# A masked-patch loss: batch sums by a 32x32 transposition and a store from four partitions, in place of a mask product

## The chip, the cores and the metric

The kernel runs on one core of a Trainium2 chip. Its engines are named as in the profile: PE (TensorE), DVE (VectorE), ACT (ScalarE), POOL (GpSimd) and SP (SyncE, which here only issues transfers). The metric is the device time of one execution in microseconds; a profile of one execution also gives the span from the first to the last instruction, which is a little shorter.

## The reference

`pred` and `target` are 32 x 147 x 768 in f32. Each row of 768 of `target` is normalised by its own mean and variance; the result is, for each of the 32 batch elements, the mean over 147 rows and 768 columns of the squared difference.

```python
mean = target.mean(axis=-1, keepdims=True)
var = target.var(axis=-1, keepdims=True)
target = (target - mean) / np.sqrt(var + 1e-6)
loss = np.mean((pred - target) ** 2, axis=-1)
return loss.mean(axis=-1).astype(np.float32)
```

## The kernel before

The rows lie on 128 partitions: partition 4*b + j holds a stretch of batch element b, so J = 4 partitions belong to one element. 147 rows are not divisible by 4: j = 0, 1, 2 hold 37 rows and j = 3 holds 36. In the code's terms a "column" c is one row of 768 on each partition; columns 0 to 35 fill 128 partitions, and the column REST = 36 exists for j = 0, 1, 2 alone and is kept packed on 96 partitions, three for each element.

Loads come in pieces, in a fixed order. The first four columns of `target` and its REST column go through SP's hardware queue in f32; all others go through POOL's software queue, which converts to bf16 on the way. `target`'s REST column is cut into five transfers:

```python
if c0 == REST and kind == "t":
    for j, b0, b1 in [(j, 0, B) for j in range(J - 2)] + [(J - 2, 0, 16), (J - 2, 16, 24), (J - 2, 24, B)]:
        pin(eng.dma_start(out=til[:n].rearrange("(b j) w -> b j w", j=J - 1)[b0:b1, j],
                          in_=bass.AP(tensor=x.tensor, offset=src.offset + b0 * N * D + j * KJ * D,
                                      ap=[[N * D, b1 - b0], [1, w]])))
else:
    pin(eng.dma_start(out=til[:n], in_=src))
```

For each column DVE takes the statistics (L164, L165), ACT the root (L188), DVE the reciprocal (L194), POOL the normalised target `s` (L214). Then the difference is formed, either by PE (minus identity times `s`, plus identity times `pred`, into PSUM, L231) or by DVE (L276), and squared and summed along the row by ACT (L260) or DVE (L280). Each such unit leaves one f32 number per partition:

```python
pin(nc.scalar.activation(out=z[:n, :w], in_=z[:n, :w], func=ACTF.Square, accum_out=dest[:n]))
...
pin(nc.vector.scalar_tensor_tensor(out=z, in0=z, scalar=1.0, in1=z, op0=ALU.mult, op1=ALU.mult, accum_out=dest))
```

The sums of the 22 early units are columns of one tile `rl`, which DVE reduces; REST's sum and those of the six last units stand alone (`finals`). PE then adds everything up across partitions: eight accumulating f32 products with a mask of 128 x 32 (96 x 32 for REST) whose entries are 1/(N*D) where the partition belongs to the element, else 0. The last of these comes when the last unit is done; the sums lie in one partition of PSUM, and are copied and stored.

```python
nc.gpsimd.memset(m, 1.0 / (N * D))          # masks(): the same for mask and mask_rest, each with
nc.gpsimd.affine_select(...)                # two selections that set the rest to 0
...
acc = psum1.tile([1, B], F32)
op("rl_sum", "DVE", 0.2, early_ops, lambda: pin(nc.vector.tensor_reduce(
    out=rl_sum, in_=rl, axis=mybir.AxisListType.X, op=ALU.add)), rank=3.0)
finals.insert(0, ("rl_sum", rl_sum, mask, P))
...
    pin(nc.tensor.matmul(acc, vec[:n], m[:n], start=len(turn) == 1, stop=len(turn) == len(finals)))
...
ob = singles.tile([1, B], F32)
pin(nc.vector.tensor_copy(out=ob, in_=acc))
nc.sync.dma_start(out=out, in_=ob[0, :])
```

The masks and identities are made by POOL at the start, ahead of its first loads. All operations are listed with estimated durations, and a small scheduler in the kernel's Python fixes their order on each engine.

Of the kernel before, what the change touches and what calls it, by code (L numbers as in the profile page):

```python
# [7 lines left out]
F32 = mybir.dt.float32  # L8
BF16 = mybir.dt.bfloat16
ALU = mybir.AluOpType  # L10
ACTF = mybir.ActivationFunctionType
# [3 lines left out]
def kernel(  # L15
# [7 lines left out]
    nc = tc.nc  # L23
    pin = tc.keep_in_program_order
    B, N, D = pred.shape
    eps = 1e-6
    P = 128
    J = P // B
    KJ = (N + J - 1) // J
    KM = N - (J - 1) * KJ  # L30
    assert KJ == KM + 1
    RP = B * (J - 1)
    half = D // 2
    BANK = 512
    REST = KM
# [4 lines left out]
    def rows_of(c):  # L40
        return RP if c == REST else P
# [5 lines left out]
    singles = ctx.enter_context(tc.tile_pool(name="singles", bufs=1))  # L47
    psum1 = ctx.enter_context(tc.tile_pool(name="psum1", bufs=1, space=bass.MemoryType.PSUM))

    stream = []
# [40 lines left out]
    def op(name, engine, dur, needs, fn, rank=0.0, early=0.0):  # L93
        by_name[name] = len(ops)
        ops.append((name, engine, dur, needs, fn, rank, early))
# [4 lines left out]
    def load(kind, c0, c1, d0, d1, q):  # L100
        x = targ_f if kind == "t" else pred_f
        n, w = rows_of(c0), d1 - d0
        til = data.tile([P, (c1 - c0) * w], BF16 if q == "sw" else F32, name=f"{kind}{c0}_{d0}")
        src = bass.AP(tensor=x.tensor, offset=x.offset + c0 * D + d0,
                      ap=[[N * D, B], [KJ * D, J - 1 if c0 == REST else J], [1, (c1 - c0) * w]])
        eng = {"hw": nc.sync, "hw2": nc.scalar, "sw": nc.gpsimd}[q]
        if c0 == REST and kind == "t":

            for j, b0, b1 in [(j, 0, B) for j in range(J - 2)] + [(J - 2, 0, 16), (J - 2, 16, 24), (J - 2, 24, B)]:
                pin(eng.dma_start(out=til[:n].rearrange("(b j) w -> b j w", j=J - 1)[b0:b1, j],  # L110
                                  in_=bass.AP(tensor=x.tensor, offset=src.offset + b0 * N * D + j * KJ * D,
                                              ap=[[N * D, b1 - b0], [1, w]])))
        else:
            pin(eng.dma_start(out=til[:n], in_=src))  # L114
        for c in range(c0, c1):
            KIND[kind].setdefault(c, []).append((d0, d1, til, (c - c0) * w))


    land, lanes, clock = {}, {"hw": [], "hw2": [], "sw": []}, 2.3
    for i, (kind, c0, c1, d0, d1, q) in enumerate(stream):  # L120
        w = (c1 - c0) * (d1 - d0)
        clock += w * rows_of(c0) / P * 0.915 / D + (0.0 if w >= 4 * D else 0.04)
        lanes[q].append(clock + 1.1)
        for c in range(c0, c1):
            land[kind, c, d0] = clock + 1.1
        k = len(lanes[q])
        op(("load", i), {"hw": "SP", "hw2": "ACT", "sw": "POOL"}[q], 0.6, [], lambda a=stream[i]: load(*a), rank=-1.0,
           early=0.0 if k <= 8 else lanes[q][k - 9] + 0.3)

    def landed(kind, c):  # L130
        return max(t for (k, cc, d), t in land.items() if k == kind and cc == c)

    ident = singles.tile([P, P], BF16)
    nident = singles.tile([P, P], BF16)
    mask = singles.tile([P, B], F32)
    mask_rest = singles.tile([P, B], F32)
    eps_t = singles.tile([P, 1], F32)

    def identities():
# [3 lines left out]
                                        base=0, pattern=[[-1, P]], channel_multiplier=1))  # L143

    def masks():
        for m, per, n in ((mask, J, P), (mask_rest, J - 1, RP)):
            pin(nc.gpsimd.memset(m, 1.0 / (N * D)))
            pin(nc.gpsimd.affine_select(out=m[:n], in_=m[:n], compare_op=ALU.is_ge, fill=0.0,  # L148
                                        base=0, pattern=[[-per, B]], channel_multiplier=1))
            pin(nc.gpsimd.affine_select(out=m[:n], in_=m[:n], compare_op=ALU.is_ge, fill=0.0,  # L150
                                        base=per - 1, pattern=[[per, B]], channel_multiplier=-1))

    op("eps", "DVE", 0.1, [], lambda: pin(nc.vector.memset(eps_t, eps)))
    op("ident", "POOL", 1.3, [], identities, rank=-2.0)
# [50 lines left out]
    def normalise(u, c):  # L205
        n = rows_of(c)
        if c == u[0]:
            s = work.tile([P, 2 * D], BF16, name="s")
            for m, cc in enumerate(u):
                sbuf[cc] = (s, m * D)  # L210
        s, so = sbuf[c]
        (_, _, til, o), = tbuf[c]
        r, nm = rs[c]
        pin(nc.gpsimd.tensor_scalar(out=s[:n, so:so + D], in0=til[:n, o:o + D], scalar1=nm, scalar2=r,  # L214
                                    op0=ALU.add, op1=ALU.mult))
# [41 lines left out]

    def square_act(u, d0, w, dest):
        n, z = rows_of(u[0]), zs[u, d0]
        pin(nc.scalar.activation(out=z[:n, :w], in_=z[:n, :w], func=ACTF.Square, accum_out=dest[:n]))  # L260

    def difference(u, d0, w):

# [13 lines left out]

    def square_dve(u, d0, w, dest):
        z = zs[u, d0][:, :w]
        pin(nc.vector.scalar_tensor_tensor(out=z, in0=z, scalar=1.0, in1=z, op0=ALU.mult, op1=ALU.mult,  # L280
                                           accum_out=dest))

    tail = 6
    n_early = len(units) - 1 - tail
    rl = singles.tile([P, n_early], F32)
    rl_sum = singles.tile([P, 1], F32)
    pairs_pe = [u for u, d0, d1, eng in units if eng == "ACT" and (u[0] == REST or len(u) * (d1 - d0) > 2 * BANK)]
    n_pairs = len(pairs_pe)
# [2 lines left out]
    finals = []  # L291
    early_ops, users, dusers, dprev, pusers, lusers, seen = [], [], [], [], [], [], set()
    for k, (u, d0, d1, eng) in enumerate(units):
        w = len(u) * (d1 - d0)
        arrive = max(t for (kk, c, d), t in land.items() if kk == "p" and c in u and d < d1)
        norms = [("norm", c) for c in u]
        for c in u:
            if c not in seen:
                op(("norm", c), "POOL", 1.02, [("recip", group_of[c])], lambda u=u, c=c: normalise(u, c), rank=k)
                seen.add(c)  # L300
        if k < len(units) - tail:
            if u[0] == REST:
                dest = singles.tile([P, 1], F32, name="rl_rest")
                finals.append((("sq", k), dest, mask_rest, RP))
            else:
                dest = rl[:, len(early_ops):len(early_ops) + 1]
                early_ops.append(("sq", k))
        else:
            dest = singles.tile([P, 1], F32, name=f"rl{k}")
            finals.append((("sq", k), dest, mask, P))  # L310
        if eng in ("DVE", "DVE+ACT"):
            op(("diff", k), "DVE", 0.57 * w / D + 0.05, norms + dusers[-5:-4] + dprev[-1:], lambda u=u, d0=d0, w=w: difference(u, d0, w), rank=-2.0,
               early=arrive)
            dusers.append(("sq", k))
            dprev.append(("diff", k))
            if eng == "DVE":
                op(("sq", k), "DVE", 1.0 * w / D, [("diff", k)],
                   lambda u=u, d0=d0, w=w, dest=dest: square_dve(u, d0, w, dest), rank=-1.0)
            else:
                op(("sq", k), "ACT", 0.65 * w / D + 0.22, [("diff", k)],  # L320
                   lambda u=u, d0=d0, w=w, dest=dest: square_act(u, d0, w, dest), rank=k)
            continue
        op(("subt", k), "PE", 0.37 * w / D, norms + (users[-2:-1] if len(users) < n_pairs else users[n_pairs - 1:n_pairs] + (pusers[-2:-1] if wide(u) else lusers[-3:-2])) + ["ident"],
           lambda u=u, d0=d0, w=w: sub_target(u, d0, w), rank=k + 0.0)
        op(("pred", k), "PE", 0.37 * w / D, [("subt", k)], lambda u=u, d0=d0, w=w: add_pred(u, d0, w), rank=k,
           early=arrive)
        op(("sq", k), "ACT", 0.65 * w / D + 0.22, [("pred", k)],
           lambda u=u, d0=d0, w=w, dest=dest: square_act(u, d0, w, dest), rank=k)
        users.append(("sq", k))
        if len(users) > n_pairs:  # L330
            (pusers if wide(u) else lusers).append(("sq", k))

    acc = psum1.tile([1, B], F32)
    op("rl_sum", "DVE", 0.2, early_ops, lambda: pin(nc.vector.tensor_reduce(
        out=rl_sum, in_=rl, axis=mybir.AxisListType.X, op=ALU.add)), rank=3.0)
    finals.insert(0, ("rl_sum", rl_sum, mask, P))
    turn = []

    def final(vec, m, n):
        turn.append(n)  # L340
        pin(nc.tensor.matmul(acc, vec[:n], m[:n], start=len(turn) == 1, stop=len(turn) == len(finals)))  # L341


    for i, (need, vec, m, n) in enumerate(finals):
        op(("final", i), "PE", 0.2, [need, "masks"], lambda v=vec, m=m, n=n: final(v, m, n), rank=90.0,
           early=max(land.values()) + 0.4)


    HOP = 0.15
# [3 lines left out]
    while left:  # L353
        best = None
        for i in left:
            name, engine, dur, needs, fn, rank, early = ops[i]
            if any(x not in end for x in needs):
                continue
            t = max([free[engine], early] + [end[x] + (0.0 if ops[by_name[x]][1] == engine else HOP) for x in needs])
# [4 lines left out]
        _, i, t = best  # L364
        name, engine, dur, needs, fn, rank, early = ops[i]
# [2 lines left out]
        order.append((t, name, engine))  # L368
        fn()

    ob = singles.tile([1, B], F32)
    pin(nc.vector.tensor_copy(out=ob, in_=acc))  # L372
    nc.sync.dma_start(out=out, in_=ob[0, :])


# [33 lines left out]
```

## Time and profile before

| | |
|---|---|
| device time, median of 3 | 76.61 us (76.5 to 76.67) |
| span of the profiled execution | 75.0 us |
| busy: DVE, POOL, ACT, PE | 55.9, 52.5, 30.7, 28.3 us |
| DMA | 15.41 MB written by the transfers, 28.90 MB read from HBM |
| mean granted clock of PE | 0.923 |

A busy time is the sum over an engine's instructions, whatever they wait for; the share of the span that it makes says how much room an engine has on average. The slices show when an engine or the DMA is busy, and the chain that ended last follows the work back from the last instruction, each time to what released it.

### The profile page before, as it was taken

Reading aid. Unit: us, or ns where it says so; the run is one execution under the profiler, and the core shown is the slowest. Engines: PE = TensorE matmul, PEld = TensorE weight load, DVE = VectorE, ACT = ScalarE, POOL = GpSimd, SP = SyncE. Lnnn points to the kernel's source line nnn. Section 1 sums busy time; section 2 is a strip of 40 time slices with the busy share of each in tenths; the row PEclk is TensorE's granted clock in tenths of the full one; section 3 lists DMA queues with packets and bytes.
Section 4 is the critical chain, followed back from the end, with each engine's and each line's share of the span. In section 5 each row is a group of like instructions: output and inputs, shape, how many; then the busy total and the mean of one; then the engine's idle time right before and its main releaser. Section 6 shows DMA issues by size and latency. Waiting matters only on the chain.

```text
span 75.0 us, 567 instructions
## 1 busy us (share of the span) xinstructions
PE 28.3 (38%) x87; PEld 8.7 (12%) x88; DVE 55.9 (74%) x154; ACT 30.7 (41%) x65; POOL 52.5 (70%) x72
## 2 busy tenths in 40 slices
PE   0000003570000000398940006897860560789650
PEld 0000000110000000123300002142220210222120
DVE  0000899999999999970899999860997579999850
ACT  5100022202002020059502020878969979985960
POOL 5899008995299939499869995982798799950000
PEclk9999999999999999999999999999999955555796
DMA  0799999999999999999999989999999999999900
GB/s 0 236 420 346 233 215 220 192 231 223 229 210 210 214 200 220 223 236 229 216 223 216 208 174 213 216 226 216 216 213 210 197 219 210 213 202 207 140 0 0
DMA packets 3301, 15.41 MB, mean 206 GB/s; under 512 B 418, under 2 KB 1154, under 8 KB 2786
## 3 DMA queue, kind: packets, MB, share of 16 engines
q0 software_dynamic: 2992, 13.52, 88.5%
q1 hardware_dynamic: 306, 1.87, 6.7%
q14 instruction: 3, 0.02, 0.1%
HBM read 28.90 MB, written 0.00 MB: 385 GB/s over the span
## 4 chain that ended last, share of the span: by engine, by line
DMA 79%; POOL 7%; ACT 5%; PE 4%; issue 1%; DVE 0%; ACTq 0%; POOLq 0%
DMA t<-in_target_dram 43%; DMA p<-in_pred_dram 36%; PE zp L231 4%; POOL t L114 3%; ACT zl L260 2%; ACT zp L260 2%; POOL p L114 1%; POOL nident L142 0%; POOL ident L142 0%; PE acc L341 0%; POOL mask L148 0%; POOL mask_rest L148 0%; POOL mask L150 0%; POOL mask_rest L150 0%; DVE ob L372 0%
## 5 line engine op out<-in xcount | busy, mean ns | idle before, releaser
L214 POOL TENSOR_SCALAR s<-t,nm,r 128x768 bf16<-128x768 bf16 (+2 forms) x37 | 39.0, 1062 | 7.1 <-DVE r L194 6.6
L164 DVE BATCH_NORM_STATS2 st<-t 128x6 f32<-128x384 bf16 (+2 forms) x74 | 36.2, 531 | 7.6 <-DMA t<-in_target_dram 7.5
L231 PE MATMUL z<-p,ident 128*128 128x512 bf16 (+2 forms) x25 | 9.3, 509 | 21.5 <-DMA p<-in_pred_dram 21.5
L231 PE MATMUL z<-s,nident 128*128 128x512 bf16 (+2 forms) x26 | 10.5, 522 | 15.2 <-POOL s L214 13.8
L188 ACT ACTIVATE r<-mv,eps_t 128x4 f32<-128x4 f32 (+2 forms) x11 | 3.2, 295 | 31.1 <-DVE mv L165 30.2
L260 ACT ACTIVATE z<-z 128x1536 f32<-128x1536 f32 (+1 forms) x9 | 12.3, 1364 | 8.1 <-PE z L231 8.1
L114 POOL DMA_DIRECT2D p<-in_pred_dram x15 | 8.5, 570 | 6.1 <-DMA t<-in_target_dram 3.9
L276 DVE TENSOR_TENSOR zd<-p,s 128x1536 bf16<-128x1536 bf16 (+3 forms) x13 | 8.6, 680 | 2.1 <-DMA p<-in_pred_dram 2.0
L165 DVE BATCH_NORM_AGGREGATE mv<-st 128x2 f32<-128x12 f32 (+1 forms) x37 | 7.7, 209 | 1.3
L231 PEld LDWEIGHTS <-ident 128*128 128x128 bf16 (+1 forms) x36 | 4.6, 127 | 34.1 <-issue 32.8
L260 ACT ACTIVATE zd<-zd 128x1536 bf16<-128x1536 bf16 (+1 forms) x5 | 6.7, 1345 | 0.6 <-DVE zd L276 0.5
L231 PEld LDWEIGHTS <-nident 128*128 128x128 bf16 (+1 forms) x36 | 3.6, 115 | 28.4 <-issue 16.8
L280 DVE SCALAR_TENSOR_TENSOR zd<-zd 128x256 bf16<-128x256 bf16 (+2 forms) x8 | 5.3, 662 | 0.2
L194 DVE RECIPROCAL r<-r 128x4 f32<-128x4 f32 (+2 forms) x11 | 1.5, 133 | 4.5 <-ACT r L188 4.5
L260 ACT ACTIVATE zp<-zp 128x1024 f32<-128x1024 f32 (+1 forms) x4 | 3.6, 899 | 1.1 <-PE zp L231 1.1
L231 PE MATMUL zp<-p,ident 128*128 128x512 bf16 x7 | 3.5, 581 | 0.9 <-DMA p<-in_pred_dram 0.9
L231 PE MATMUL zp<-s,nident 128*128 128x512 bf16 x7 | 2.7, 484 | 2.5 <-ACT z L260 2.5
L114 POOL DMA_DIRECT2D t<-in_target_dram x6 | 3.6, 623 | 0.0
L231 PE MATMUL zl<-s,nident 128*128 128x512 bf16 x3 | 1.8, 585 | 3.5 <-POOL s L214 3.5
L189 ACT ACTIVATE nm<-mv 128x4 f32<-128x4 f32 (+2 forms) x11 | 2.1, 189 | 0.0
L260 ACT ACTIVATE zl<-zl 128x512 f32<-128x512 f32 x3 | 1.8, 585 | 0.0
L231 PE MATMUL zl<-p,ident 128*128 128x512 bf16 x3 | 1.6, 531 | 0.4 <-DMA p<-in_pred_dram 0.4
(29 smaller groups left out, 10.5 us busy)
## 6 DMA issues: line engine op xcount, KB each, us to landing
t<-in_target_dram POOLq DMA_DIRECT2D x4, 768.0 KB, 13.4
t<-in_target_dram POOLq DMA_DIRECT2D x2, 1536.0 KB, 27.1
p<-in_pred_dram POOLq DMA_DIRECT2D x4, 768.0 KB, 38.7
t<-in_target_dram SPq DMA_DIRECT2D x1, 1536.0 KB, 6.9
p<-in_pred_dram POOLq DMA_DIRECT2D x1, 1536.0 KB, 38.7
p<-in_pred_dram POOLq DMA_DIRECT2D x4, 384.0 KB, 29.9
p<-in_pred_dram POOLq DMA_DIRECT2D x3, 192.0 KB, 15.7
t<-in_target_dram SPq DMA_DIRECT2D x2, 96.0 KB, 6.6
```

Source lines behind the costliest of these rows:

```text
L114: pin(eng.dma_start(out=til[:n], in_=src))
L164: pin(nc.vector.bn_stats(out=st[:n, j, :], in_=x))
L165: pin(nc.vector.bn_aggr(out=out, in_=st[:n, :len(parts)]))
L188: pin(nc.scalar.activation(out=r[:n], in_=mv[:n, :, 1], func=ACTF.Sqrt, bias=eps_t[:n], scale=1.0))
L189: pin(nc.scalar.activation(out=nm[:n], in_=mv[:n, :, 0], func=ACTF.Copy, scale=-1.0))
L194: pin(nc.vector.reciprocal(out=rs[g][:n], in_=rs[g][:n]))
L214: pin(nc.gpsimd.tensor_scalar(out=s[:n, so:so + D], in0=til[:n, o:o + D], scalar1=nm, scalar2=r, op0=ALU.add, op1=ALU.mult))
L231: pin(nc.tensor.matmul(z[:n, zo + a:zo + b], eye[:n, :n], src[:n, o + a:o + b], start=first, stop=not first))
L260: pin(nc.scalar.activation(out=z[:n, :w], in_=z[:n, :w], func=ACTF.Square, accum_out=dest[:n]))
L276: pin(nc.vector.tensor_tensor(out=x, in0=y, in1=v, op=ALU.subtract))
L280: pin(nc.vector.scalar_tensor_tensor(out=z, in0=z, scalar=1.0, in1=z, op0=ALU.mult, op1=ALU.mult, accum_out=dest))
```

## The change

It does six things. The mask product over partitions goes. In its place every unit's sums stay one number per partition; POOL adds the early sum and four of the late ones, DVE adds the two last in one instruction into the first column of a zeroed 128 x 32 tile, transposes this in 32 x 32 blocks, so that the 32 numbers of each block lie side by side in one partition (0, 32, 64, 96), and sums groups of J = 4. Eight results lie in each of four partitions and are stored from there. REST's sums, packed three to an element on 96 partitions, are moved by one PE product to three of the four partitions of their element and become one more column of `rl`. The factor 1/(N*D) goes from the masks into the squares (its root as ACT's scale, itself as DVE's scalar). The mask for REST becomes 128 wide, and the other mask goes. And `target`'s REST column is loaded by one transfer.

It is meant to put a short chain on one engine at the end, in place of PE, PSUM and a copy.

```diff
-        if c0 == REST and kind == "t":
-
-            for j, b0, b1 in [(j, 0, B) for j in range(J - 2)] + [(J - 2, 0, 16), (J - 2, 16, 24), (J - 2, 24, B)]:
-                pin(eng.dma_start(out=til[:n].rearrange("(b j) w -> b j w", j=J - 1)[b0:b1, j],
-                                  in_=bass.AP(tensor=x.tensor, offset=src.offset + b0 * N * D + j * KJ * D,
-                                              ap=[[N * D, b1 - b0], [1, w]])))
-        else:
-            pin(eng.dma_start(out=til[:n], in_=src))
+        pin(eng.dma_start(out=til[:n], in_=src))
...
-    mask = singles.tile([P, B], F32)
-    mask_rest = singles.tile([P, B], F32)
+    mask_rest = singles.tile([P, P], F32)
+    flat = singles.tile([P, 32], F32)
...
-        for m, per, n in ((mask, J, P), (mask_rest, J - 1, RP)):
-            pin(nc.gpsimd.memset(m, 1.0 / (N * D)))
-            (two selections for each)
+        pin(nc.gpsimd.memset(mask_rest, 1.0))
+        for base, sign in ((0, -1), (J - 2, 1)):
+            pin(nc.gpsimd.affine_select(out=mask_rest[:RP], in_=mask_rest[:RP], compare_op=ALU.is_ge, fill=0.0,
+                                        base=base, pattern=[[sign * (J - 1), P]], channel_multiplier=-sign * J))
+        pin(nc.gpsimd.memset(flat, 0.0))
...
-        ... func=ACTF.Square, accum_out=dest[:n]))
+        ... func=ACTF.Square, scale=mean ** 0.5, accum_out=dest[:n]))
...
-        ... scalar=1.0, in1=z, op0=ALU.mult, op1=ALU.mult,
+        ... scalar=mean, in1=z, op0=ALU.mult, op1=ALU.mult,
...
-    acc = psum1.tile([1, B], F32)
+    acc = psum1.tile([P, 1], F32)
+    op("rest", "PE", 0.3, [rest[0], "masks"], lambda: pin(nc.tensor.matmul(
+        acc, mask_rest[:RP], rest[1][:RP], start=True, stop=True)), rank=90.0)
+    op("rest_sum", "DVE", 0.15, ["rest"], lambda: pin(nc.vector.tensor_copy(out=rl[:, n_early:], in_=acc)), rank=4.0,
+       early=landed("t", KM - 1) + 2.0)
...
-    for i, (need, vec, m, n) in enumerate(finals):
-        op(("final", i), "PE", 0.2, [need, "masks"], lambda v=vec, m=m, n=n: final(v, m, n), rank=90.0,
-           early=max(land.values()) + 0.4)
+        pin(nc.gpsimd.tensor_tensor(out=s, in0=total[1], in1=vec, op=ALU.add))     # in add(vec)
+    for i, (need, vec) in enumerate(finals[:-2]):
+        op(("add", i), "POOL", 0.2, [need, total[0]], lambda v=vec: add(v), rank=91.0)
+        total[0] = ("add", i)
...
-    ob = singles.tile([1, B], F32)
-    pin(nc.vector.tensor_copy(out=ob, in_=acc))
-    nc.sync.dma_start(out=out, in_=ob[0, :])
+    pin(nc.vector.scalar_tensor_tensor(out=flat[:, 0:1], in0=finals[-2][1], scalar=total[1], in1=finals[-1][1],
+                                       op0=ALU.add, op1=ALU.add))
+    rows = singles.tile([P, 32], F32)
+    pin(nc.vector.transpose(rows, flat))
+    ob = singles.tile([P, 32 // J], F32)
+    pin(nc.vector.tensor_reduce(out=ob, in_=rows.rearrange("p (b j) -> p b j", j=J), axis=mybir.AxisListType.X, op=ALU.add))
+    nc.sync.dma_start(out=out.rearrange("(q b) -> q b", q=P // 32), in_=ob[::32])
```

In the order of instructions nothing else moves: PE gets REST's product ahead of the products with the fifth to eighth columns of `pred` and loses the eight at the end, DVE gets a copy ahead of its first difference and three operations in place of one at the end, POOL four additions at the end, and SP issues one load in place of five. ACT's order is the same.

More of the change, by code (lines that the diff above doesn't have):

```diff
@@ L48 @@
     psum1 = ctx.enter_context(tc.tile_pool(name="psum1", bufs=1, space=bass.MemoryType.PSUM))
+    mean = 1.0 / (N * D)
     stream = []
@@ L145, in masks @@
     def masks():
-        for m, per, n in ((mask, J, P), (mask_rest, J - 1, RP)):
-            pin(nc.gpsimd.memset(m, 1.0 / (N * D)))
[L148 to L151, printed above, removed]
+        pin(nc.gpsimd.memset(mask_rest, 1.0))
[3 more added lines that the diff above has]
+        pin(nc.gpsimd.memset(flat, 0.0))
     op("eps", "DVE", 0.1, [], lambda: pin(nc.vector.memset(eps_t, eps)))
@@ L259, in square_act @@
         n, z = rows_of(u[0]), zs[u, d0]
-        pin(nc.scalar.activation(out=z[:n, :w], in_=z[:n, :w], func=ACTF.Square, accum_out=dest[:n]))
+        pin(nc.scalar.activation(out=z[:n, :w], in_=z[:n, :w], func=ACTF.Square, scale=mean ** 0.5,
+                             accum_out=dest[:n]))
     def difference(u, d0, w):
@@ L279, in square_dve @@
         z = zs[u, d0][:, :w]
-        pin(nc.vector.scalar_tensor_tensor(out=z, in0=z, scalar=1.0, in1=z, op0=ALU.mult, op1=ALU.mult,
+        pin(nc.vector.scalar_tensor_tensor(out=z, in0=z, scalar=mean, in1=z, op0=ALU.mult, op1=ALU.mult,
                                            accum_out=dest))
@@ L284 @@
     n_early = len(units) - 1 - tail
-    rl = singles.tile([P, n_early], F32)
+    rl = singles.tile([P, n_early + 1], F32)
     rl_sum = singles.tile([P, 1], F32)
@@ L303 @@
                 dest = singles.tile([P, 1], F32, name="rl_rest")
-                finals.append((("sq", k), dest, mask_rest, RP))
+                rest = (("sq", k), dest)
             else:
@@ L309 @@
             dest = singles.tile([P, 1], F32, name=f"rl{k}")
-            finals.append((("sq", k), dest, mask, P))
+            finals.append((("sq", k), dest))
         if eng in ("DVE", "DVE+ACT"):
@@ L331, with add @@
             (pusers if wide(u) else lusers).append(("sq", k))
-    acc = psum1.tile([1, B], F32)
-    op("rl_sum", "DVE", 0.2, early_ops, lambda: pin(nc.vector.tensor_reduce(
-        out=rl_sum, in_=rl, axis=mybir.AxisListType.X, op=ALU.add)), rank=3.0)
[L336 to L341, printed above, removed]
-    for i, (need, vec, m, n) in enumerate(finals):
-        op(("final", i), "PE", 0.2, [need, "masks"], lambda v=vec, m=m, n=n: final(v, m, n), rank=90.0,
-           early=max(land.values()) + 0.4)
+    acc = psum1.tile([P, 1], F32)
[3 more added lines that the diff above has]
+       early=landed("t", KM - 1) + 2.0)
+    op("rl_sum", "DVE", 0.2, early_ops + ["rest_sum"], lambda: pin(nc.vector.tensor_reduce(
+        out=rl_sum, in_=rl, axis=mybir.AxisListType.X, op=ALU.add)), rank=3.0)
+    total = ["rl_sum", rl_sum]
+    def add(vec):
+        s = singles.tile([P, 1], F32, name=f"sum{len(total)}")
+        pin(nc.gpsimd.tensor_tensor(out=s, in0=total[1], in1=vec, op=ALU.add))
+        total[1] = s
+        total.append(s)
+    for i, (need, vec) in enumerate(finals[:-2]):
+        op(("add", i), "POOL", 0.2, [need, total[0]], lambda v=vec: add(v), rank=91.0)
+        total[0] = ("add", i)
     HOP = 0.15
```

## The prediction

> **What bounds the kernel now.** I read four views: the 40 slices and the queue table, the chain that ended last, the order of time over the last 10 us, and the shapes of the small instructions. The slices and the queue table come first.
>
> ```profile
> PEclk9999999999999999999999999999999955555796
> DMA  0799999999999999999999989999999999999900
> GB/s 0 236 420 346 233 215 220 192 231 223 229 210 210 214 200 220 223 236 229 216 223 216 208 174 213 216 226 216 216 213 210 197 219 210 213 202 207 140 0 0
> ...
> q0 software_dynamic: 2992, 13.52, 88.5%
> q1 hardware_dynamic: 306, 1.87, 6.7%
> ```
>
> The 16 DMA engines are at 90% or more from the third slice (3.75 us) to 71 us. VectorE is busy 74% and GpSimd 70%, so they have room on average. The chain that ended last says the same: 79% of it is DMA.
>
> ```profile
> 6.37 32.00 DMA t<-in_target_dram
> 38.36 0.29 issue
> 38.65 27.21 DMA p<-in_pred_dram
> 65.86 0.04 issue
> 65.90 2.88 PE zp L231 x6
> ...
> 68.86 1.11 ACT zp L260 x2
> 69.97 1.72 ACT zl L260 x6
> 71.69 0.04 issue
> 71.73 0.58 ACT zp L260
> ```
>
> So the time is: a start that fills the DMA queues, about 65 us in which bytes flow, and a tail. The tail is where most of the edits are, so I look at its last instructions.
>
> ```profile
> 71.66 0.29 DVE L276 TENSOR_TENSOR zd<-p,s 128x256 bf16<-128x256 bf16 x1 [0.21 <-DMA p<-in_pred_dram]
> ...
> 72.23 0.20 ACT L260 ACTIVATION_READ_ACCUMULATOR zp<-zp 128x1 f32 x1
> 72.33 0.08 DVE L280 DVE_READ_ACCUMULATOR zd<-zd 128x1 f32 x1
> 72.47 0.14 PEld L341 LDWEIGHTS acc<-mask,rl 128*1 128x1 f32 x4 [0.50 <-ACT zp L260]
> 72.48 0.28 PE L341 MATMUL acc<-mask,rl 128*1 128x32 f32 x4 [0.37 <-ACT zp L260]
> 72.79 0.18 DVE L372 COPY ob<-acc 1x32 f32<-1x32 f32 x1 [0.38 <-PE acc L341]
> 73.00 0.26 SPq L373 DMA_DIRECT2D out_dram<-ob  x1
> ```
>
> Two paths finish within 0.02 us of each other: ScalarE's last square (sum read out at 72.43) and VectorE's last square (72.41), which began when the last piece of `pred` landed. From 72.43 to the store's issue at 73.00 is 0.57 us; from there to the end of the span (75.0) is the store's own 2.0 us.
>
> **What the Trainium skill says.** "DMA: Bandwidth & Descriptors", section "Why a DMA increments its semaphore by 16 and not by 1": a transfer runs on the largest k up to 16 that divides the slowest dimension on both sides, on the hardware queue on the lowest-numbered k engines, and each of these posts one completion. The trace agrees in its count: 128 + 96 rows of `target`, 16 + (16+16+16+8+8) completions, one packet and one completion of the store make 306, the figure of q1. The same page, "Anatomy of one DMA", puts most of a small transfer's 2 us into the write receipt; the 2.0 us from issue to end agree. "VectorE: DVE Perf Modes", "The three transpose paths": VectorE's transposition works in separate 32x32 blocks and takes 311 ns for 128x128 bf16; no run here shows one yet. "SBUF — State Buffer", "Who interferes with whom": VectorE in its two-port modes and GpSimd lock each other out for whole instructions. That fits L214 here, 970 ns at least and 2847 at most.
>
> **Part 1, the tail.** Removed: the eight f32 mask products, six of which ran beside other work; on the path were only the last two (72.43 to 72.77, hop included) and the copy out of PSUM (to 72.97). Added, one after the other on VectorE:
>
> - hop from ScalarE: 0.04, as PE had (72.43 to 72.47);
> - the three-operand sum on 128x1: no such row; the reciprocal of 96x1 took 105 ns, I take 0.10;
> - the transposition of 128x32: an estimate from that page's 311 ns for four times the columns and from the 105 ns floor of the smallest operations: 0.15;
> - the reduction 128x32 to 128x8: the 128x22 reduction took 176 ns, I take 0.18;
> - two gaps of 0.04 between dependent operations (the difference ends 71.95, its square starts 71.98), and 0.03 to SyncE.
>
> Sum 0.04 + 0.10 + 0.15 + 0.18 + 0.08 + 0.03 = 0.58, against 0.57. No gain: +0.01.
>
> Beside it are four GpSimd additions. The last two wait for ScalarE's third-last sum, read out at 71.77. A GpSimd memset of 128x1 takes 93 ns and a select of 128x32 212, with gaps of 0.07 between dependent ones, so I take 0.15 + 0.07 each: 71.82 + 0.44 = 72.26, which leaves 0.17 before 72.43. Hidden, but not by much.
>
> **Part 2, the store.** One packet of 128 bytes becomes four of 32 on four engines. I keep the 2.0 us and add 0.05 for the slowest of four and a longer issue. +0.05.
>
> **Part 3, REST's sums moved by PE.** The order of instructions puts the product behind the fourth unit's subtractions, where PE next waits for p4 (PE's waits on `pred` are 21.5 us in all), and the copy out of `acc` ahead of the difference of p16, where VectorE idled 0.55 us for DMA (56.17 to 56.72). Both fit in. 0.
>
> **Part 4, the factor in the squares.** An immediate in the same instructions. 0.
>
> **Part 5, the start.** GpSimd's mask work ran 1.83 to 3.14 us. Now: a memset of 128x128 (0.20 for bf16), two selects of 96x128 (0.29 each from the 128x128 identities), a memset of 0.12, and gaps: about 1.05, so the first software load goes out some 0.25 us sooner. The DMA share was 0.86 in 2 to 4 us and 0.96 in 4 to 6 us by the windows, on the hardware queue alone, so the engines were not waiting for it. 0 to -0.05; I take 0.
>
> **Part 6, `target`'s REST column as one load.** SyncE issues once (0.68) in place of five times (3.35 us), and VectorE reads this column only at 12.40, long after either lands. What changes is the share of each engine. By the rule above, pieces of 32, 32, 16, 8 and 8 rows give engines 0 to 7 seven rows each and engines 8 to 15 five; one load of 96 gives all six. A row costs an engine 6.7% of 16 x 75 us = 80 us, over 1.87 MB, times 3,072 bytes = 0.13 us. The packet records of the trace show that t4's last packets start from 10.92 to 11.43 us over the 16 engines, and the two latest of these engines are not among those that carried the pieces of eight rows. So the engines 8 to 15 hold the end, and each gets one row more: +0.10 to +0.13, carried through to the last landing since every engine is full until 71 us. I take +0.10.
>
> **Sum:** 0.01 + 0.05 + 0.10 = +0.16 on 76.61, rounded to 76.75 us.
>
> **The rivals.** (a) The transposition is cheap and so is the reduction (0.08 to 0.12 us each), the store is no slower and the balance of engines doesn't matter: then the tail gives 0.15 and the time is 76.4. For it speaks that a small reciprocal takes 105 ns where this copy out of PSUM takes 179; against it that three dependent steps stand where two stood. (b) The lagging engine at the end is one of 0 to 7, which now lose a row and four completions: then the stream ends up to 0.15 earlier, 76.45. The packet records at 11 us speak against. (c) GpSimd's additions become the bound: each 0.3 us in place of 0.15, or locked out by VectorE's last difference at 71.66. Then the sum comes after 72.5 and the time is 76.9 to 77.0. (d) The issue and receipt of a store on four partitions costs 0.3 us more: 77.0. SyncE's loads took 577 to 732 ns to issue against 258 for this store, so the shape matters to an unknown degree.
>
> **Range and chances.** All effects are of 0.05 to 0.4 us; 2% is 1.5 us, and nothing here can reach it, as the DMA stream of some 65 us moves the same bytes. (a) and (b) together would make 76.3, (c) and (d) together 77.2. I predict 76.75, 76.3 to 77.15 as the range, and give 0.02 to faster, 0.95 to within 2%, 0.03 to slower.
>
> **What would show it.** Right: q1 with 264 packets (224 rows, 32 completions, 4 + 4 of the store); VectorE's three last operations within 0.5 to 0.6 us after ScalarE's last sum; the GpSimd additions over by 72.3; the last `pred` landing 0.1 us later against the start of the span, and so the last difference. Wrong: a wait of VectorE's sum on GpSimd, a transposition of over 0.25 us, over 2.2 us from store to end, or a last landing that comes sooner.

## The result, and the profile after

The changed kernel takes 77.49 us (median of 6; 77.39 of the four that the ratio counts), the kernel before 76.59 us; the ratio is 1.0108, with a 95% interval of 1.0088 to 1.0129. So it is slower by 0.83 us (0.0108 x 76.6), where the prediction said 0.16. Some executions, of the kernel before too, take 1 to 2 us longer than the rest (in their traces PE's granted clock is at half until 71.0 to 72.2 us, in the other traces until 69.6 to 70.5 us); the ratios leave them out as far as they could be told apart, and two runs (a3_dvesum, b1_again) had no others.

The span of the profiled execution grew from 75.0 to 75.6 us. First the slices and the queue table of the changed kernel (packets, megabytes, share of 16 engines).

```profile
PEclk9999999999999999999999999999999755555985
DMA  0899999999999999999999999999999999999400
GB/s 0 234 416 346 245 211 221 193 233 211 224 221 221 205 209 260 215 215 208 208 215 208 208 216 211 211 208 218 215 215 218 201 210 216 213 200 203 72 0 0
...
q0 software_dynamic: 2992, 13.52, 87.7%
q1 hardware_dynamic: 264, 1.87, 6.7%
```

The stream has the same shape and the same bytes. q1 has the 264 packets that were foretold (224 rows, 32 completions, four packets and four completions of the store). Next the chain that ended last (start, length in us, what).

```profile
6.08 32.09 DMA t<-in_target_dram
38.17 0.29 issue
38.45 27.20 DMA p<-in_pred_dram
65.66 0.04 issue
65.70 2.87 PE zp L225 x6
...
72.11 0.11 ACTq L409
72.22 0.02 issue
72.25 0.05 DVEq L372
72.30 0.06 issue
72.36 0.23 DVE flat L372
72.59 0.02 issue
72.61 0.22 DVE rows L375
72.83 0.02 issue
72.86 0.18 DVE ob L377
```

Up to the tail this execution is 0.2 us ahead of the one before: DMA hands over at 65.66, where it was 65.86. All the loss comes after that. The last instructions in order of time, still of the changed kernel:

```profile
71.38 0.19 ACT L254 ACTIVATION_READ_ACCUMULATOR zl<-zl 128x1 f32 x1
71.44 0.29 DVE L271 TENSOR_TENSOR zd<-p,s 128x256 bf16<-128x256 bf16 x1 [0.20 <-DMA p<-in_pred_dram]
...
71.71 0.54 POOL L340 TENSOR_TENSOR sum<-sum,rl 128x1 f32<-128x1 f32 x2 [0.16 <-ACT zl L254]
...
72.02 0.19 ACT L254 ACTIVATION_READ_ACCUMULATOR zp<-zp 128x1 f32 x1
72.12 0.08 DVE L275 DVE_READ_ACCUMULATOR zd<-zd 128x1 f32 x1
72.36 0.22 DVE L372 SCALAR_TENSOR_TENSOR flat<-rl,sum,rl 128x1 f32<-128x1 f32 x1
72.61 0.21 DVE L375 STREAM_TRANSPOSE rows<-flat 128x32 f32<-128x32 f32 x1
72.86 0.18 DVE L377 TENSOR_REDUCE ob<-rows 128x8 f32<-128x32 f32 x1
73.07 0.64 SPq L378 DMA_DIRECT2D out_dram<-ob  x1
```

Three things are to be read here. ScalarE's last sum is out at 72.21 (72.02 + 0.19), and the store is issued at 73.07: 0.86 us, where it was 0.57. GpSimd's last addition ends at 72.25, 0.04 us after ScalarE's sum, and VectorE's sum begins at 72.36; the 0.11 us between are steps of VectorE's own instruction queue (0.05 and 0.06 in the chain). The chain of this trace comes to VectorE from ScalarE, that of a1_store1 from GpSimd, so which of the two holds VectorE last is a matter of a few hundredths of a us. And the store's issue takes 0.64 us where it took 0.26, and the span ends 2.5 us after it began (75.6 - 73.07), where it was 2.0. So in this pair of executions -0.2 (stream), +0.29 (from the last sum to the issue) and +0.53 (store) make +0.6.

### The profile page after: what moved, and what is told of

The parts are those of the page before. It is cut to its first block, busy times and chain, and to the rows that moved or that the text cites. A ratio compares the mean times of both kernels' runs of the same rounds, so it can differ in the third digit from the quotient of the medians.

```text
span 75.6 us, 538 instructions
## 1 busy us (share of the span) xinstructions
PE 27.4 (36%) x73; PEld 8.6 (11%) x74; DVE 56.1 (74%) x157; ACT 30.7 (41%) x65; POOL 53.2 (70%) x74
## 4 chain that ended last, share of the span: by engine, by line
DMA 78%; POOL 7%; ACT 5%; PE 4%; issue 1%; DVE 1%; ACTq 0%; POOLq 0%; DVEq 0%
DMA t<-in_target_dram 42%; DMA p<-in_pred_dram 36%; PE zp L225 4%; POOL t L108 3%; ACT zl L254 2%; ACT zp L254 2%; POOL p L108 1%; POOL mask_rest L143 1%; POOL nident L136 0%; POOL ident L136 0%; DVE flat L372 0%; DVE rows L375 0%; DVE ob L377 0%; POOL mask_rest L141 0%; POOL nident L135 0%
## 5 line engine op out<-in xcount | busy, mean ns | idle before, releaser
L225 PE MATMUL z<-s,nident 128*128 128x512 bf16 (+2 forms) x25 | 10.0, 513 | 14.9 <-POOL s L208 13.5
```

Of the source, the lines that this page charges most:

```text
L225: pin(nc.tensor.matmul(z[:n, zo + a:zo + b], eye[:n, :n], src[:n, o + a:o + b], start=first, stop=not first))
```

## Experiments

Each time is compared with that of the kernel before on the same chip. "Changed" and "before" name the kernel that was edited.

### a1_store1: the changed kernel, stored from one partition

The sums of the first eight elements go into the zeroed tile, and one row of it is stored. The other 24 sums are left out.

```diff
-    ob = singles.tile([P, 32 // J], F32)
-    pin(nc.vector.tensor_reduce(out=ob, ...))
-    nc.sync.dma_start(out=out.rearrange("(q b) -> q b", q=P // 32), in_=ob[::32])
+    pin(nc.vector.tensor_reduce(out=flat[:, 0:32 // J], ...))
+    nc.sync.dma_start(out=out.rearrange("(q b) -> q b", q=1), in_=flat[::128, 0:32])
```

> The changed kernel, but the store takes 32 numbers from one partition (the first eight sums and zeros; the other 24 sums are left out). Theory S (the store's shape costs most): the span from the store's issue to the end falls from 2.5 to 2.0 us and its issue from 0.64 to 0.26 us, so the time falls from some 77.4 to 76.9 us. Theory C (the chain of VectorE at the end costs all of it, and the longer store is an effect of what is queued): the issue stays near 0.64 us and the time at 77.4.

Measured: a ratio of 1.0042 (1.0007 to 1.0076), which is 0.5 us below the changed kernel's 1.0108; of the nine executions behind it seven took 76.70 to 77.11 us and two 77.7. In its trace, in order of time:

```profile
73.62 0.22 DVE L372 SCALAR_TENSOR_TENSOR flat<-rl,sum,rl 128x1 f32<-128x1 f32 x1 [0.36 <-POOL sum L340]
73.87 0.21 DVE L375 STREAM_TRANSPOSE rows<-flat 128x32 f32<-128x32 f32 x1
74.12 0.19 DVE L376 TENSOR_REDUCE flat<-rows 128x8 f32<-128x32 f32 x1
74.40 0.29 SPq L377 DMA_DIRECT2D out_dram<-flat  x1
```

The operations on VectorE take the same, and the issue is 0.29 us again; the span ends at 76.3, 1.9 us after the issue began. Theory S holds. The edit also stores from another tile (`flat`), but a_store2 below does so too and pays the long issue. The first line names the releaser of the three-operand sum: GpSimd.

### b_store4: the reverse, on the kernel before

The mask product and its copy stay, but eight sums go into a zeroed tile of 128 x 8 and four partitions of it are stored; 24 sums are left out.

```diff
-    ob = singles.tile([1, B], F32)
-    pin(nc.vector.tensor_copy(out=ob, in_=acc))
-    nc.sync.dma_start(out=out, in_=ob[0, :])
+    pin(nc.vector.tensor_copy(out=ob4[0:1, :], in_=acc[:, 0:8]))      # ob4: 128 x 8, zeroed at the start
+    nc.sync.dma_start(out=out.rearrange("(q b) -> q b", q=4), in_=ob4[::32])
```

> The kernel before, its mask product and copy kept, but the copy takes eight of the 32 sums into a tile of 128 x 8 and the store takes four partitions of it (24 sums are left out and zeros stored for them). If the store's shape alone costs 0.5 us, as the one-partition store in the changed kernel says, this rises from 76.6 to 77.15 us, with an issue of 0.6 us in place of 0.26. If the store is dear only after the transposition, it stays at 76.6.

Measured: 1.0104 (1.0024 to 1.0183), a wide interval that holds the expected 1.007: one of its four executions took 78.20 us, the others 77.11 to 77.55. The trace is sharper:

```profile
72.48 0.28 PE L342 MATMUL acc<-mask,rl 128*1 128x32 f32 x4 [0.36 <-ACT zp L261]
72.80 0.15 DVE L372 COPY ob<-acc 1x8 f32<-1x8 f32 x1 [0.37 <-PE acc L342]
72.98 0.55 SPq L373 DMA_DIRECT2D out_dram<-ob  x1
```

Everything up to the store is as before, to 0.02 us (issued at 72.98, before at 73.00), and the span ends at 75.5 instead of 75.0. The store's shape alone costs 0.5 us, without transposition or GpSimd additions. Source and destination change together in these runs; which of the two sides makes the cost was not tested.

### a_store2 and a_store16: how the cost goes with the rows

The same edit as a1_store1 with two partitions of 16 numbers, and with 16 partitions of two (sums left out).

> The changed kernel with a store of 16 numbers from each of two partitions (sums left out). If every shape of more than one row costs the same: issue 0.6 us, issue to end 2.5 us, as with four. If it goes by rows, 0.26 + (0.64 - 0.26) / 3 = 0.39 us for the issue.

> The changed kernel with a store of two numbers from each of 16 partitions (sums left out). If every shape of more than one row costs the same: issue 0.6 us. If it goes by rows: 0.26 + 15 x 0.13 = 2.2 us. [...]

Each was executed once. The instruction of the store (line, engine, duration in ns least/median/most, start) for two rows and then for 16:

```profile
L377 SPq DMA_DIRECT2D out_dram<-flat x1: 618/618/618, 73.2 to 73.2; - x1
```

```profile
L377 SPq DMA_DIRECT2D out_dram<-flat x1: 545/545/545, 73.3 to 73.3; - x1
```

Two rows cost 0.62 us, 16 rows 0.55, four rows 0.64 (the changed kernel) and 0.55 (b_store4). From issue to the end it is 2.45 us with two rows (75.7 - 73.25) and 2.6 with 16. It is a step between one row and more than one, and not a price for each row.

### a3_dvesum and a3_again: the changed kernel without GpSimd's additions

All late sums become columns of one tile, and one VectorE reduction over seven columns takes the place of four additions and the three-operand sum.

```diff
-            dest = singles.tile([P, 1], F32, name=f"rl{k}")
+            dest = late[:, 1 + len(finals):2 + len(finals)]       # rl_sum is late[:, 0:1]
...
-    for i, (need, vec) in enumerate(finals[:-2]):
-        op(("add", i), "POOL", ...)
...
-    pin(nc.vector.scalar_tensor_tensor(out=flat[:, 0:1], in0=finals[-2][1], scalar=total[1], in1=finals[-1][1], ...))
+    pin(nc.vector.tensor_reduce(out=flat[:, 0:1], in_=late, axis=mybir.AxisListType.X, op=ALU.add))
```

> The changed kernel without the four GpSimd additions and without the sum of three operands: the late sums are columns of one tile, and one VectorE reduction over seven columns gives the first column of the tile that is transposed. If the wait for GpSimd costs 0.1 us and the pointer operands make the sum 0.22 instead of 0.18 us, the time falls by 0.10 to 0.15 us to some 77.25. If the end is set by ScalarE's last sum alone, it stays at 77.4.

Measured: 78.43 to 79.28 us in six executions, a ratio of 1.0258 (1.0220 to 1.0297), which for the reason given with the result says nothing of the edit. The same kernel again:

> The same kernel as the one with VectorE's reduction over seven late columns[...]. In its first trace the way from ScalarE's last sum to the store's issue was 0.69 us, against 0.86 in the changed kernel; if that is a gain of the end, the time is 77.4 - 0.17 = 77.2 us. If something else sets the end, 77.4.

Measured: 1.0064 (1.0036 to 1.0092) from two executions, 77.21 and 77.22 us; the expected 77.2. The traced execution took 79.26 us. Its end:

```profile
74.15 0.18 ACT L254 ACTIVATION_READ_ACCUMULATOR zp<-zp 128x1 f32 x1
74.37 0.16 DVE L370 TENSOR_REDUCE flat<-late 128x1 f32<-128x7 f32 x1 [0.29 <-ACT zp L254]
74.56 0.21 DVE L372 STREAM_TRANSPOSE rows<-flat 128x32 f32<-128x32 f32 x1
74.81 0.19 DVE L374 TENSOR_REDUCE ob<-rows 128x8 f32<-128x32 f32 x1
75.03 0.64 SPq L375 DMA_DIRECT2D out_dram<-ob  x1
```

From 74.33 to 75.03 it is 0.70 us in place of 0.86: the hop is 0.04 in place of 0.15, and the sum 0.16 in place of 0.22. VectorE now waits for ScalarE. The store is unchanged, at 0.64. A nearer partner is the traced execution of a2_rest5 (below), which took 79.44 us and has GpSimd's additions and the three-operand sum:

```profile
74.24 0.18 ACT L261 ACTIVATION_READ_ACCUMULATOR zp<-zp 128x1 f32 x1
74.53 0.22 DVE L379 SCALAR_TENSOR_TENSOR flat<-rl,sum,rl 128x1 f32<-128x1 f32 x1 [0.36 <-POOL sum L347]
...
75.24 0.55 SPq L385 DMA_DIRECT2D out_dram<-ob  x1
```

There the hop is 0.11 and the whole 0.82 us. So the saving is 0.12 to 0.16 us: 0.07 to 0.11 in the hop and 0.06 in the sum. The two were taken together, so the run does not part the need to wait for GpSimd from the three-operand form. The interval (1.0036 to 1.0092) overlaps that of the changed kernel, so this step rests on the trace more than on the time.

### a3_store1: both taken away

The edits of a3_dvesum and a1_store1 together; 24 sums are left out.

> Both causes taken away: VectorE's reduction over the late columns, and a store from one partition (24 of the 32 sums left out, zeros stored). If the store's shape (0.55) and the wait and pointer sum (0.17) add up, 77.4 - 0.72 = 76.7 us, level with the kernel before (76.6 to 76.7). If a third loss is left, 76.9 or more.

Measured: 1.0011 (0.9996 to 1.0026), from eleven executions. The two causes add up: 1.0108 less 0.0097, which is 0.74 us of the 0.83. Its trace has at the end:

```profile
74.25 0.18 ACT L254 ACTIVATION_READ_ACCUMULATOR zp<-zp 128x1 f32 x1
...
75.19 0.30 SPq L374 DMA_DIRECT2D out_dram<-flat  x1
```

What is left of the time is 0.2 us at most, and fits the 0.19 us by which this chain (74.43 to 75.19, 0.76) is still longer than PE's (0.57).

### a2_rest5, b1_rest1, b1_again: target's REST column in one load or five

The changed kernel with the five pieces back (a2_rest5), and the kernel before with the one load and nothing else (b1_rest1, and again b1_again).

> The changed kernel with the five pieces of target's REST column back. My prediction said that the single load costs 0.10 us; then the last landing comes 0.1 us sooner and the time is 77.3. The rival, from the trace (last landing 0.2 us sooner with the single load, counted from the start of the span): the single load gains; then the time rises by 0.1 to 0.2 us to some 77.6. A third: the earlier start of the software loads made the gain; then it stays at 77.4.

> The kernel before with the single load of target's REST column and nothing else. If the single load gains: 0.1 to 0.2 us less than before (76.4 to 76.5), with the last landing of pred sooner by as much. If it costs, as I predicted: 76.7. If only the earlier start of the software loads counts: 76.6, no difference.

> The kernel before with the single load (six rows on every engine), beside the skewed one on the same chip. My prediction: 0.10 us over before (a ratio of 1.0013). Its first measurement leaned the other way (0.9985, with 1.0017 still inside). If the balance of rows counts and the lower engines hold the end: 0.9983. If it doesn't count: 1.000.

Measured: 1.0135 (1.0096 to 1.0174) for a2_rest5, whose interval overlaps that of the changed kernel; 0.9985 (0.9953 to 1.0017) for b1_rest1; b1_again, the same kernel, gave 1.0157 (1.0107 to 1.0206), all six executions at 77.59 us or more, where eight of the nine behind the 0.9985 took 76.36 to 76.79; it is set aside. My +0.10 us (1.0013) and a gain as large are both inside 0.9953 to 1.0017, that is a gain of 0.36 us to a cost of 0.13. The traces lean to a gain: the last packet of the software queue ends at 71.06 to 71.39 us in nine traces with one load (mean 71.18; c1_rest1_late is left out, as its start differs) and at 71.23 to 71.30 in three with five pieces (mean 71.27). So the sign of the one load stays open, and the 0.2 us by which the stream of the changed kernel ended sooner than that of the kernel before lies within the scatter of the single-load traces.

### b_rest_skew: the imbalance made larger

Nine pieces: 32 rows, then eight of eight rows.

```diff
-            for j, b0, b1 in [(j, 0, B) for j in range(J - 2)] + [(J - 2, 0, 16), (J - 2, 16, 24), (J - 2, 24, B)]:
+            for j, b0, b1 in [(0, 0, B)] + [(j, b, b + 8) for j in range(1, J - 1) for b in range(0, B, 8)]:
```

> The kernel before with target's REST column in nine pieces: 32 rows, and eight of eight rows. By the rule that my prediction used, engines 0 to 7 get ten rows each and engines 8 to 15 two, in place of seven and five. If the share of rows is carried to the last landing, as I predicted, the engines 0 to 7 lag by 3 x 0.13 = 0.4 us more, the last landing comes some 0.3 us later and the time is 76.9 to 77.0. If the balance of these rows doesn't reach the end, it is 76.6 to 76.7 as before.

Measured: 1.0102 (1.0056 to 1.0148), some 0.8 us (0.4 to 1.1) in place of the expected 0.3 to 0.4. Two views of its trace, the order of time at the end and on VectorE at the start:

```profile
71.99 0.29 DVE L276 TENSOR_TENSOR zd<-p,s 128x256 bf16<-128x256 bf16 x1 [0.21 <-DMA p<-in_pred_dram]
...
73.33 0.26 SPq L373 DMA_DIRECT2D out_dram<-ob  x1
```

```profile
14.91 1.02 DVE L164 BATCH_NORM_STATS2 st<-t 96x6 f32<-96x384 f32 x2 [2.41 <-DMA t<-in_target_dram]
```

The last landing, and with it the last difference, is 0.33 us later than before (71.99 against 71.66), as expected of the share of rows; the last packet of the software queue ends at 71.60 us, later than in any other trace. But the run is not clean: the column also landed so late that VectorE stood for 2.41 us, and the span ends 2.3 us after the store's issue, where it was 2.0. There SyncE's nine closing waits show: in the trace of the kernel before eight are over by 73.8 us and the ninth ends with the store's landing at 74.1; here three are over by 73.8 us, and six follow the landing, from 74.4 to 74.8 us. So this run agrees with the balance reaching the end, and can't show it alone.

### c1_rest1_late: a version that was to beat both

The kernel before with the single load, and the masks made behind the first eight software loads.

```diff
-    op("masks", "POOL", 1.3, [], masks, rank=-2.0)
+    op("masks", "POOL", 1.3, [], masks, rank=-0.5, early=6.2)
```

> A version meant to beat both: the kernel before with the single load of target's REST column, and its masks made behind the first eight software loads in place of ahead of them. If the stream began late for want of software loads: 0.3 us less than before (76.3). If the first packets of those loads wait for the hardware queue's own data anyhow (in the trace they start at 6.8 to 7.0 us, when the first load's data is through, whether issued from 3.1 or from 2.8 us): as with the single load alone, 76.5 to 76.6.

Measured: 1.001 (0.996 to 1.006). No gain shows: six of the eight executions took 76.56 to 76.76 us, though the interval just reaches the hoped-for 0.3 us. GpSimd and VectorE in its order of time:

```profile
1.84 1.23 POOL L107 DMA_DIRECT2D t<-in_target_dram  x2
```

```profile
8.46 1.02 DVE L157 BATCH_NORM_STATS2 st<-t 128x6 f32<-128x384 f32 x2 [7.53 <-DMA t<-in_target_dram]
```

The software loads go out at 1.84 in place of 3.09 us, and the first statistics start at 8.46 in place of 7.70. By the packet records the first packet of the software queue starts at 6.03 us; it was 6.97 before, and 6.83 in the changed kernel (issued at 2.76). That is 3.9 to 4.2 us behind the issue in all three: issued 1.25 us sooner than before, the first packet came 0.94 us sooner. So my expectation that these packets wait for the first load's data was wrong; in this trace they run among those of the first load, which lands later (the first statistics start 0.76 us later).

## Why the prediction was wrong

- **What bounds the kernel, and where the change acts: right.** The stream is untouched and the tail decides; the effect stays under 2%. (One slice of DMA before shows an 8, so "90% or more" holds for all but that one.)
- **Part 2, the store: wrong, and it is the step that failed most.** "I keep the 2.0 us and add 0.05 for the slowest of four and a longer issue." It is +0.5, shown from both sides: one row in the changed kernel takes 0.5 away, four rows in the kernel before put it on. I had the hint in hand under rival (d) (loads with many rows took 577 to 732 ns to issue, the store of one row 258) and kept it as a rival of 0.3 us, though it was the only measured price of a shape of several rows. By the packet records the first packet leaves 0.73 us after the issue began with one row and 1.24 with four; 0.38 of these 0.51 us are the longer issue. From the first packet to the end of the span it is 1.25 and 1.28 us, so the cost lies ahead of the first packet and not in the landing. Nor is the 2.0 us all "the store's own": SyncE's wait for the landing is over 1.1 us after the issue began (1.6 to 1.7 with four rows), and the last 0.9 us of the span are the closing steps of the program.
- **Part 1, the chain of VectorE: right in kind, wrong in size.** The sum of terms was 0.58 and is 0.86 us. The sum of three operands, put at 0.10 from a reciprocal, took 0.22; the transposition, put at 0.15, took 0.21 (the Trainium skill, "VectorE: DVE Perf Modes", section "The three transpose paths", has 311 ns for 128x128 in bf16; the 128x32 in f32 here took 213, far more than a quarter of it); the reduction took 0.18 as said; and the hop of 0.04 became 0.15, of which 0.04 is GpSimd's later end and 0.11 VectorE's own start.
- **GpSimd's additions, "hidden, but not by much": wrong by a little.** I put 0.49 us between the sum of ScalarE that the last two wait for (its last but one, which the prediction calls the third-last) and the end of the last addition (71.77 to 72.26); it was 0.68 (71.57 to 72.25), as the first began 0.14 after the sum and the two took 0.54 in place of 0.44. ScalarE's last sum came 0.64 us after that one. So rival (c) is true in kind, and 0.1 us at most in size. That rival thought of a lock-out by VectorE: L214's three long executions (1.48, 1.83 and 2.85 us) do run beside VectorE's differences and squares, which read two tensors, but no run shows which mode these are in.
- **Parts 3 and 4: right so far as the trace tells.** VectorE's copy of REST's sums took 104 ns at 55.9 us and left 0.56 us of waiting for DMA behind it, and PE's product ran at 38 us, far from the tail.
- **Part 5: right so far as seen.** The loads went out 0.3 us sooner; c1_rest1_late moved them by more, and no gain shows.
- **Part 6: open.** +0.10 us is inside the interval, and so is a gain of that size, to which the traces lean. b_rest_skew agrees that the share of rows reaches the end. That engines 8 to 15 held the end is not shown, as the packet records name no engine.

So the prediction was off through two terms: the store (0.05 for 0.5) and the chain (0.01 for 0.29). With these measured, and nothing for Part 6, the sum is 76.6 + 0.5 + 0.29 = 77.4 us, which is what was found.

## What to carry to other kernels

Judge a short chain of instructions at the end together with the transfer that follows it: here a result laid out in one row was worth 0.5 us, more than any instruction of the chain took. Price an unknown shape from the nearest row of the profile with that shape, here the loads of many rows, and not from the same statement in the old shape. And give a tiny operation its measured price: the three in a row took 0.18 to 0.22 us each here and did not beat PE's two products and a copy.

## What the runs showed of the hardware that was not expected

- SyncE's issue of a store of 128 bytes took 0.26 to 0.30 us from one partition and 0.55 to 0.65 us from 2, 4 or 16. Counted from the start of the issue, the first packet left after 0.71 to 0.73 us against 1.18 to 1.24, and the span ended after 1.9 to 2.0 us (2.3 in b_rest_skew) against 2.45 to 2.6.
- On VectorE 128x1 with two tensor operands and a per-partition scalar took 219 ns, a reduction of 128x7 to 128x1 some 160 ns, and the transposition of 128x32 in f32 213 ns. GpSimd's sum of two 128x1 tiles took 189 to 269 ns.
- The first packet of a software load left 3.9 to 4.2 us after the first issue, whether that came at 1.84, 2.76 or 3.09 us.
